# Token-major products with up to 512 columns from several column ranges, one PSUM bank for each token tile

## The chip, the cores and the metric

The kernel runs on one core of one Trainium2 chip. The metric is the device time of one execution in microseconds (us). A core has TensorE (PE in the profile; PEld are its weight loads), VectorE (DVE), ScalarE (ACT), GpSimd (POOL), and SyncE (SP), which here starts weight transfers.

## What is computed

Two blocks of two layers each, over 512 tokens of width 1024, batch 1. All arithmetic is float32 in the reference. Cut to what matters here:

```python
def first_block(x, ...):          # "layer A", twice
    for l in range(DEPTH):
        h = rms_norm(x, norm_g[l])
        p = h @ w_in[l]
        (cb, cc, cx, cgate, q, k, v, agate, iq, ik, iw, pu, pgate, mgate) = split_columns(p)
        y_a = short_conv_mixer(...)
        y_b = sparse_attention_mixer(q, k, v, agate, iq, ik, iw, ...)   # q, k: rms_norm per head of 64, then rope
        y_c = pool_mixer(...)
        x = x + merged @ w_o[l]

def second_block(x, mem, ...):    # "layer B" twice, each with cross attention and an MLP behind it
    for i in range(DEPTH):
        hn = rmsnorm(h, ln_mix[i])
        (aq, ak, av, hy, gq, gk, gv, go, glr, gates) = split_cols(hn @ w_in[i], IN_SPLITS_2)
        y_a = attention_mixer(aq, ak, av, ...) @ w_br_attn[i]
        y_b = hyena_mixer(hy, ...) @ w_br_hyena[i]
        y_c = gla_mixer(gq, gk, gv, go, glr, ...) @ w_br_gla[i]
        h = h + mixed @ w_out[i]
        h = h + memory_cross_attention(rmsnorm(h, ln_x[i]), rmsnorm(mem, ln_mem[i]), ...)
        h = h + jnp.square(jax.nn.relu(rmsnorm(h, ln_mlp[i]) @ mlp_w1[i])) @ mlp_w2[i]
```

The low-rank rows `glr` are 32 columns of layer B's input product; they give the decay of the gated linear attention (GLA).

## The kernel before

Every float32 product is made of three matmuls: both operands are split into a high part H and a remainder L, and `mm3` (L242 to L244) adds H·H, H·L and L·H in one PSUM bank. Weights are brought in pieces of four k-tiles (128 rows each) and 256 columns by `wload`: one transfer on SP into a raw buffer (`wr`, three of them), then ScalarE writes H (`wh`, three) and VectorE writes L (`wl`, two), 1024 columns at a time.

There are two forms of product. `gemm_t` keeps weights stationary and moves 512 tokens: its result has features on the partitions. `gemm_m` keeps tokens stationary and moves 256 weight columns: its result has tokens on the partitions ("token-major"), as queries, keys and values need it for norms and rope. A PSUM bank holds 512 float32 values per partition, so `gemm_m` puts two token tiles of 256 columns in one bank, and four token tiles take two banks. The pool `mm` has four banks, and each 256-column piece of either form takes two of them; while one piece's two banks are evicted, the next piece fills the other two.

Layer A (`layer_a`) makes the index queries with `gemm_m` (L642 and L644 in the listing), then in two chunks c the queries, keys and values by `q`, `k`, `v`; these products are put between others (`half`, and `between` in `gate_out`). `ev_q` and `ev_k` evict two token tiles at once: `sums64` squares on ScalarE and sums on VectorE, `rsqrt_small` takes the power -1/2 on GpSimd, `rope` runs on VectorE (L484, L486, L487), `split_hl` writes H and L. `ev_k` normalises first and turns afterwards (L675), so it waits for GpSimd.

Layer B starts with five token-major products in the order keys and values, q, half of the GLA values, q, the other half. `norm_full`, which scales the transposed input by the row norm, is queued behind the fourth. Then come weight-stationary products for the Hyena branch, interleaved with attention, and behind them the 32-column low-rank product (`ev_lr`), `gla_begin` (the decay), a 512-column product, and the GLA heads, which run as a background generator: `gla_steps` advances by one step at each half of a product, and `starts` says at which step each head begins. `gla_begin` begins with a memset (L1451); a head's first TensorE work are transposes of `kl`, written at L1521.

The cross attention makes keys and values of the 256 memory tokens (two token tiles) with `gemm_m`, four pieces of 256 columns each.

The code gives the operations and priorities; a scheduler of the framework then sets each engine's order when the kernel is built, by priority among what it holds ready. Weight loads and evictions have raised priority. `run_later` runs what was queued for the end of a product, as the turning of the cross keys.

Of the kernel before, what the change touches and what calls it, by code (L numbers as in the profile page):

```python
# [10 lines left out]
F32 = mybir.dt.float32  # L11
# [120 lines left out]
class Kernel:  # L132
# [309 lines left out]
    def rope_tables(self, base, g=None, axial=False):  # L442
# [3 lines left out]
        tb = self.tp.tile([P, 512], F32, tag="rt", name=self.nm("rt"), bufs=2)  # L446
        Atab = tb[:, : NT * 64].rearrange("p (t d) -> p t d", t=NT)
        Btab = tb[:, NT * 64 :].rearrange("p (t d) -> p t d", t=NT)
# [73 lines left out]
    def sums64(self, dst, src, nh):  # L522

        nc = self.nc
        sq = self.s2()[:, : 2 * nh * 64].rearrange("p (t h d) -> p t h d", t=2, h=nh)
        nc.scalar.activation(sq, src, AF.Square)
        nc.vector.tensor_reduce(dst, sq, AX.X, ALU.add)
# [65 lines left out]
    def layer_a(self, l, st, next_norm, side=None):  # L593
# [61 lines left out]
        def qkv(c):  # L655
# [5 lines left out]
            def ev_q(_, w, t, ps):  # L661
                src = ps.rearrange("p t (h d) -> p t h d", h=4)
                self.sums64(sigv[:, t : t + 2], src, 4)
                r = self.s2().rearrange("p (t h d) -> p t h d", t=2, h=4)
                self.rope(r, src, tabs_q, t, 4)
                self.split_hl(hls[0], r, t)

            def ev_k(_, w, t, ps):
                src = ps.rearrange("p t (h d) -> p t h d", h=4)
                sg = self.small(8, "sgk")  # L670
                sgv = sg.rearrange("p (t h) -> p t h", t=2)
                self.sums64(sgv, src, 4)
                self.rsqrt_small(sg, sg, 1.0 / 64, 8)
                kn = self.s2().rearrange("p (t h d) -> p t h d", t=2, h=4)
                nc.vector.tensor_tensor(kn, src, sgv.unsqueeze(3).to_broadcast([P, 2, 4, 64]), ALU.mult)  # L675
                r = self.s2().rearrange("p (t h d) -> p t h d", t=2, h=4)
                self.rope(r, kn, tabs_k, t, 4)
                self.split_hl(hls[1], r, t)
# [144 lines left out]
        half(1, [lambda: None] + steps)  # L823
# [430 lines left out]
    def layer_b(self, l, st, spec, next_norm):  # L1254
# [13 lines left out]
        tabs_q = self.rope_tables(self.axial_base, gains[:, 0:64], True)  # L1268
        tabs_k = self.rope_tables(self.axial_base, gains[:, 64:128], True)

        hlv = lambda t: t.rearrange("p a b -> p (a b)").rearrange("p (t h z d) -> p t h z d", t=NT, h=4, z=2)
        qhl, sigs = [], []
        kv = hlv(self.big())

        def sigma(dst, src, t, nt, nh, mul):

            bc = lambda a: a[:, t : t + nt].unsqueeze(2).to_broadcast([P, nt, nh])
            d3 = dst.rearrange("p (t h) -> p t h", t=nt)
            nc.vector.tensor_tensor(d3, src, bc(r2), ALU.mult)
            self.rsqrt_small(dst, dst, 1.0 / 64, nt * nh)  # L1280
            nc.vector.scalar_tensor_tensor(d3, d3, mul, bc(rstd), ALU.mult, ALU.mult)

        def ev_q(c, w, t, ps):
            if t == 0:
                qhl.append(hlv(self.big()))
                sigs.append(self.small(NT * 4, "sig"))
            src = ps.rearrange("p t (h d) -> p t h d", h=4)
            ss = self.small(8, "sgk")
            ssv = ss.rearrange("p (t h) -> p t h", t=2)
            self.sums64(ssv, src, 4)  # L1290
            sigma(sigs[-1][:, t * 4 : t * 4 + 8], ssv, t, 2, 4, 0.125)
            r = self.s2().rearrange("p (t h d) -> p t h d", t=2, h=4)
            self.rope(r, src, tabs_q, t, 4, True)
            self.split_hl(qhl[-1], r, t)

        def ev_kv(c, w, t, ps):
            src = ps[:, :, 0:P].rearrange("p t (h d) -> p t h d", h=2)
            ss = self.small(4, "sgk")
            ssv = ss.rearrange("p (t h) -> p t h", t=2)
            self.sums64(ssv, src, 2)  # L1300
            sigma(ss, ssv, t, 2, 2, 1.0)
            kn = self.s2()[:, :256].rearrange("p (t h d) -> p t h d", t=2, h=2)
            nc.vector.tensor_tensor(kn, src, ssv.unsqueeze(3).to_broadcast([P, 2, 2, 64]), ALU.mult)
# [94 lines left out]
        def ev_lr(j, w, ps):  # L1398
            for i in range(2):
                nc.scalar.activation(glr[i * 32 : i * 32 + 32], ps[:32], AF.Copy)  # L1400
# [438 lines left out]
```

## Time and profile before

| | us |
|---|---|
| median of 3 runs (lowest, highest) | 3375.7 (3374.16, 3376.68) |
| the profiled execution | 3377.46 |
| its span in the profile | 3375.7 |
| mean granted TensorE clock | 0.996 |
| VectorE busy | 2326.8 |

The span is the time from the first to the last profiled instruction. The granted clock is a share of full speed, 2.4 GHz. In a row of the timeline the first number is the start, the second the duration, and a bracket tells how long the engine was idle before and what released it. Matmuls are pipelined: a row's duration is longer than the distance to the next start.

### The profile page before, as it was taken

The page shows a single profiled execution, that of the slowest core. Times are in us where ns is not written, and L with a number is a line of the kernel's source. Part 1 is how long each engine was busy: PE and PEld are TensorE (multiplying, and loading weights), DVE is VectorE, ACT ScalarE, POOL GpSimd, SP SyncE. Part 2 cuts the span into 40 slices and gives each one's busy share as a digit, 9 for nine tenths or more (in the row PEclk, how much of TensorE's full clock was granted, in tenths as well). Part 3 has the DMA queues.
Part 4 walks back from the last instruction along what each step waited for, and adds up shares of the span by engine and source line. Part 5 has one row for each costly group of instructions (what it writes and reads, how often), then busy time and mean ns, then how long its engine had stood idle before and what let it go on. Part 6 is the DMA issues. An engine that isn't in the chain of part 4 may idle for free. (4 is left out here: it accounts for less than half of the span.)

```text
span 3375.7 us, 44852 instructions
## 1 busy us (share of the span) xinstructions
PE 3322.7 (98%) x16960; PEld 2774.1 (82%) x16960; DVE 2326.8 (69%) x4307; ACT 1484.0 (44%) x2455; POOL 301.2 (9%) x472
## 2 busy tenths in 40 slices
PE   8999999999999999999999999999999999999999
PEld 6888888888777887788888888889778888888887
DVE  7966645976778778778766666866876876653354
ACT  6254433435644356533344443344663334433222
POOL 1000000010111110011011101101000101000000
PEclk9999999999999999999999999999999999999999
DMA  5322334332345432235453434433222655233332
GB/s 138 94 76 75 89 112 130 84 95 69 89 118 153 145 80 74 80 100 172 137 177 96 130 123 126 142 120 99 77 80 68 179 149 173 94 125 95 99 114 88
DMA packets 331096, 376.36 MB, mean 111 GB/s; under 512 B 22558, under 2 KB 296852, under 8 KB 330880
## 3 DMA queue, kind: packets, MB, share of 16 engines
q1 hardware_dynamic: 298496, 294.72, 29.3%
q0 software_dynamic: 32384, 78.78, 8.0%
q8 instruction: 133, 2.18, 0.3%
q14 instruction: 83, 0.68, 0.1%
HBM read 340.93 MB, written 32.51 MB: 111 GB/s over the span
## 5 line engine op out<-in xcount | busy, mean ns | idle before, releaser
L242 PE MATMUL mm<-big,wh 128*128 128x512 f32 (+1 forms) x3496 | 1373.7, 393 | 5.7 <-ACT big L220 2.5
L243 PE MATMUL mm<-big,wh 128*128 128x512 f32 (+1 forms) x3496 | 1370.7, 392 | 2.3 <-DVE big L221 2.3
L244 PE MATMUL mm<-big,wl 128*128 128x512 f32 (+1 forms) x3496 | 1368.6, 392 | 0.0
L220 ACT ACTIVATE wh<-wr 128x1024 fp32r<-128x1024 f32 (+2 forms) x528 | 551.3, 1044 | 740.0 <-PE mm L243 516.7
L221 DVE TENSOR_TENSOR wl<-wr,wh 128x1024 fp32r<-128x1024 f32 (+2 forms) x528 | 635.1, 1203 | 291.7 <-PE mm L244 203.8
L242 PEld LDWEIGHTS mm<-big,wh 128*128 128x128 f32 (+1 forms) x3496 | 656.1, 188 | 150.1 <-ACT big L220 4.4
L243 PEld LDWEIGHTS mm<-big,wh 128*128 128x128 f32 (+1 forms) x3496 | 656.5, 188 | 141.7 <-DVE big L221 5.7
L244 PEld LDWEIGHTS mm<-big,wl 128*128 128x128 f32 (+1 forms) x3496 | 656.1, 188 | 137.1 <-issue 1.0
L242 PE MATMUL mm<-wh,big 128*128 128x256 f32 x1056 | 300.4, 284 | 0.0
L243 PE MATMUL mm<-wl,big 128*128 128x256 f32 x1056 | 299.9, 284 | 0.0
L244 PE MATMUL mm<-wh,big 128*128 128x256 f32 x1056 | 299.2, 283 | 0.0
L243 PEld LDWEIGHTS mm<-wl,big 128*128 128x128 f32 x1056 | 202.2, 191 | 1.1 <-DVE wl L221 0.2
L242 PEld LDWEIGHTS mm<-wh,big 128*128 128x128 f32 x1056 | 202.1, 191 | 0.9
L244 PEld LDWEIGHTS mm<-wh,big 128*128 128x128 f32 x1056 | 202.1, 191 | 0.2
L220 ACT ACTIVATE big<-s 128x512 fp32r<-128x512 f32 (+2 forms) x196 | 99.9, 530 | 150.3 <-DVE s L487 87.1
L221 DVE TENSOR_TENSOR big<-s,big 128x512 fp32r<-128x512 f32 (+2 forms) x196 | 107.3, 568 | 18.7 <-ACT big L220 17.0
L1749 DVE TENSOR_TENSOR s<-s 128x512 f32<-128x512 f32 x64 | 43.7, 688 | 103.2 <-ACT s L1748 103.2
L221 DVE TENSOR_TENSOR pt<-sd,pt 128x512 fp32r<-128x512 f32 (+3 forms) x160 | 87.8, 551 | 23.2 <-ACT pt L220 22.4
L220 ACT ACTIVATE pt<-sd 128x512 fp32r<-128x512 f32 (+3 forms) x160 | 76.8, 489 | 61.4 <-PE sd L307 49.3
L914 DVE TENSOR_TENSOR x<-mm,x 128x512 f32<-128x512 f32 x48 | 33.0, 688 | 76.9 <-PE mm L244 76.9
L307 PE MATMUL sd<-c,p 128*128 128x128 f32 x480 | 80.8, 278 | 2.9 <-DVE sm L565 1.2
L1748 ACT ACTIVATE s<-mm 128x512 f32<-128x512 f32 x64 | 37.5, 590 | 102.2 <-PE mm L244 102.2
(423 smaller groups left out, 3967.9 us busy)
## 6 DMA issues: line engine op xcount, KB each, us to landing
wr<-in_w_in_dram SPq DMA_DIRECT2D x244, 512.0 KB, 3.7
wr<-in_mlp_w_dram SPq DMA_DIRECT2D x128, 512.0 KB, 3.6
res<-x POOLq DMA_DIRECT2D x64, 256.0 KB, 2.9
x<-res POOLq DMA_DIRECT2D x48, 256.0 KB, 3.1
F<-spec SPq DMA_DIRECT2D x36, 256.0 KB, 3.7
wr<-in_w_o_dram SPq DMA_DIRECT2D x16, 512.0 KB, 3.5
wt<-in_c_dftf_dram POOLq DMA_DIRECT2D x32, 256.0 KB, 5.0
spec<-p POOLq DMA_DIRECT2D x32, 256.0 KB, 2.7
```

The source lines that it names most:

```text
L220: nc.scalar.activation(H, src, AF.Copy)
L221: nc.vector.tensor_tensor(L, src, H.bitcast(F32), ALU.subtract)
L242: mm(out, aH, bH, start=first, stop=False, **kw)
L243: mm(out, aH, bL, start=False, stop=False, **kw)
L244: mm(out, aL, bH, start=False, stop=last, **kw)
L307: self.nc.tensor.transpose(dst_ps[: s.shape[-1], i * P : i * P + s.shape[0]], s, self.ident)
L914: self.nc.vector.tensor_tensor(X, ps, X, ALU.add)
L1748: nc.scalar.activation(a, ps, AF.Relu)
L1749: nc.vector.tensor_tensor(a, a, a, ALU.mult)
```

## The change

A new `gemm_wide` takes a list of column ranges, together up to 512 columns, and gives each token tile a bank of its own: four token tiles take all four `mm` banks, two take two. A load (`wload_wide`) brings two of the eight k-tiles at full width, with one transfer for each range. For each load the code goes through the token tiles one by one. Evictions are called for one token tile after the other.

In layer A queries and keys of a chunk become one product (256 and 256 columns); one rope turns both from the raw product, and the keys are scaled by their norm afterwards. Values stay as they are. In layer B the five products become three: q with keys and values; q with half of the GLA values; the other half with the 32 low-rank columns (288 in all). The separate low-rank product goes; its rows, token-major, are turned by four transposes. `norm_full` is queued so that it comes one hand-over later than the next. The GLA heads start at steps 0, 5, 8, 11, and step 3 is skipped as well. In the cross attention keys and values are made in two pieces of 512 columns each. The diff, cut:

```diff
+    def wload_wide(self, segs, k0):
+        nc = self.nc
+        v = lambda t: t.rearrange("p a b -> p (a b)").rearrange("p (k n) -> p k n", k=2)
+        raw = v(self.wp.tile([P, 4, 256], F32, tag="wr", name=self.nm("wr"), bufs=3))
+        H = v(self.wp.tile([P, 4, 256], F32R, tag="wh", name=self.nm("wh"), bufs=3))
+        L = v(self.wp.tile([P, 4, 256], F32R, tag="wl", name=self.nm("wl"), bufs=2))
+        with self.tc.high_priority(offset=31000):
+            o = 0
+            for ap, c, w in segs:
+                nc.sync.dma_start(raw[:, :, o : o + w],
+                                  ap[k0 * P : (k0 + 2) * P, c : c + w].rearrange("(k p) n -> p k n", p=P))
+                o += w
+            self.split(H[:, :, :o], L[:, :, :o], raw[:, :, :o])
+        return H, L
+    def gemm_wide(self, segs, stat, evac, ntok=NT):
+        w = sum(s[2] for s in segs)
+        ps = [self.ps_mm() for _ in range(ntok)]
+        for kq in range(0, KD, 2):
+            H, L = self.wload_wide(segs, kq)
+            for t in range(ntok):
+                for k in range(2):
+                    aH, aL = stat(kq + k, t)
+                    self.mm3(ps[t][:, :w], aH, aL, H[:, k, :w], L[:, k, :w], kq + k == 0, kq + k == KD - 1)
+            if kq == KD // 2 - 2:
+                self.step_background()
+                self.run_later()
+        self.step_background()
+        self.run_later()
+        with self.tc.high_priority(offset=30000):
+            for t in range(ntok):
+                evac(t, ps[t])
...
+    def rope_pair(self, n, tag):
+        tb = [self.tp.tile([P, NT * n * 64], F32, tag=tag, name=self.nm("rt"), bufs=2) for _ in range(2)]
+        return [t.rearrange("p (t g d) -> p t g d", t=NT, g=n) for t in tb]
...
+            tabs_qk = self.rope_pair(2, "rt")
+            for i in range(2):
+                self.rope_tables(self.rope_base, gains[:, i * 64 : i * 64 + 64], into=[tb[:, :, i] for tb in tabs_qk])
...
+            def ev_qk(t, ps):
+                src = ps.rearrange("p (g h d) -> p g h d", g=2, h=4)
+                ss = self.small(8, "sgk")
+                self.sums64(ss, ps)
+                self.rsqrt_small(ss, ss, 1.0 / 64, 8)
+                nc.vector.tensor_scalar(sigv[:, t], ss[:, 0:4], 0.125, None, ALU.mult)
+                r = self.s2().rearrange("p (g h d) -> p g h d", g=2, h=4)
+                self.rope(r, src, [tb[:, t] for tb in tabs_qk], 0, 4)
+                nc.vector.tensor_tensor(r[:, 1], r[:, 1], ss[:, 4:8].unsqueeze(2).to_broadcast([P, 4, 64]), ALU.mult)
+                for i in range(2):
+                    self.split(hls[i][:, t, :, 0], hls[i][:, t, :, 1], r[:, i])
...
-            def q():
-                self.gemm_m(W, 2048 + c * 256, 256, KD, h_t, ev_q)
-                self.rsqrt_small(sig, sig, 1.0 / 64, NT * 4)
-                nc.vector.tensor_scalar(sig, sig, 0.125, None, ALU.mult)
-            k = lambda: self.gemm_m(W, 2560 + c * 256, 256, KD, h_t, ev_k)
+            qk = lambda: self.gemm_wide([(W, 2048 + c * 256, 256), (W, 2560 + c * 256, 256)], h_t, ev_qk)
             v = lambda: self.gemm_m(W, 3072 + c * 256, 256, KD, h_t, ev_v)
-            return [q, k, v], (hls, sigv)
+            return [qk, v], (hls, sigv)
...
-        half(1, [lambda: None] + steps)
+        half(1, [lambda: None, steps[0], lambda: None, steps[1]])
...
+        tabs = self.rope_pair(3, "rt3")
+        for i, o in enumerate((0, 0, 64)):
+            self.rope_tables(self.axial_base, gains[:, o : o + 64], True, into=[tb[:, :, i] for tb in tabs])
...
+        def heads(c, t, ps, ng):
+            n = ng * 2
+            src = ps[:, : n * 64]
+            ss = self.small(8, "sgk")[:, :n]
+            self.sums64(ss, src)
+            nc.vector.tensor_scalar(ss, ss, r2[:, t : t + 1], None, ALU.mult)
+            self.rsqrt_small(ss, ss, 1.0 / 64, n)
+            rs = rstd[:, t : t + 1]
+            nc.vector.tensor_scalar(sigs[c][:, t * 4 : t * 4 + 4], ss[:, :4], rs, 0.125, ALU.mult, ALU.mult)
+            v = lambda x: x.rearrange("p (g h d) -> p g h d", g=ng, h=2)
+            r = self.s2()[:, : n * 64]
+            self.rope(v(r), v(src), [tb[:, t, :ng] for tb in tabs], 0, 2, True)
+            r = r.rearrange("p (h d) -> p h d", h=n)
+            self.split(qhl[c][:, t, :, 0], qhl[c][:, t, :, 1], r[:, :4])
+            if n > 4:
+                nc.vector.tensor_scalar(ss[:, 4:6], ss[:, 4:6], rs, None, ALU.mult)
+                nc.vector.tensor_tensor(r[:, 4:6], r[:, 4:6], ss[:, 4:6].unsqueeze(2).to_broadcast([P, 2, 64]), ALU.mult)
+                self.split(kv[:, t, 0:2, 0], kv[:, t, 0:2, 1], r[:, 4:6])
...
-        self.gemm_m(W, 512, 256, KD, xg_t, ev_kv)
...
-        self.gemm_m(W, 0, 256, KD, xg_t, ev_q)
-        self.gemm_m(W, 2816, 256, KD, xg_t, ev_gv)
-        self.gemm_m(W, 256, 256, KD, xg_t, ev_q)
-        self.later.append(lambda: self.norm_full(st))
-        self.gemm_m(W, 3072, 256, KD, xg_t, lambda c, *a: ev_gv(c + 256, *a))
...
+        def ev_gl(t, ps):
+            rs = rstd[:, t : t + 1]
+            nc.scalar.activation(gv[:, t, 256:512], ps[:, 0:256], AF.Copy, scale=rs)
+            for i in range(2):
+                nc.scalar.activation(lr[:, t, i * 32 : i * 32 + 32], ps[:, 256:288], AF.Copy, scale=rs)
+            nc.vector.scalar_tensor_tensor(lr[:, t, 64:96], ps[:, 256:288], rs, lr[:, t, 0:32].bitcast(F32),
+                                           ALU.mult, ALU.subtract)
+        self.gemm_wide([(W, 0, 256), (W, 512, 256)], xg_t, ev_qkv)
+        self.gemm_wide([(W, 256, 256), (W, 2816, 256)], xg_t, ev_qg)
+        self.defer(lambda: self.norm_full(st), 2)
+        self.gemm_wide([(W, 3072, 256), (W, 3840, 32)], xg_t, ev_gl)
...
-        def ev_lr(j, w, ps):
-            for i in range(2):
-                nc.scalar.activation(glr[i * 32 : i * 32 + 32], ps[:32], AF.Copy)
-            nc.vector.tensor_tensor(glr[64:96], ps[:32], glr[:32].bitcast(F32), ALU.subtract)
+        def turn_lr():
+            tp = self.ps_sd()
+            self.transposes(tp, [lr[:, t].bitcast(F32) for t in range(NT)])
+            nc.scalar.copy(glr[:96], tp[:96])
...
-            self.gemm_t(W, 3840, 32, KD, h, ev_lr)
+            turn_lr()
...
-        starts, heads, n = (0, 4, 7, 10), [], 0
+        starts, heads, n = (0, 5, 8, 11), [], 0
         while n <= starts[-1] or heads:
             if n in starts:
                 heads.append(self.gla_head(starts.index(n), b, on, qk, gv, onrm, zt))
-            if n not in (1, 2):
+            if n not in (1, 2, 3):
...
+            self.gemm_wide([(A["x_wk_2"][l], c * 512, 512)], m_t, ev_k, NM)
+        keys(0)
+        keys(1)
...
-        self.gemm_m(A["x_wv_2"][l], 0, D, KD, m_t, ev_v, ntok=NM)
+        for c in range(2):
+            self.gemm_wide([(A["x_wv_2"][l], c * 512, 512)], m_t, partial(ev_v, c), NM)
```

## Rows read from the trace of the kernel before

**Rows 1.** Part 1 of the page: engine, busy us, share of the span, instructions.
```profile
PE 3322.7 (98%) x16960; PEld 2774.1 (82%) x16960; DVE 2326.8 (69%) x4307; ACT 1484.0 (44%) x2455; POOL 301.2 (9%) x472
```

**Rows 2.** Waits of TensorE: tile and line, releaser: us, times, longest.
```profile
PE sd L307 <- DVE gl L1521: 6.8, 2, 3.4
...
PE mm L242 <- ACT big L220: 2.5, 5, 0.9
```

**Rows 3.** Windows: stretch, length, busy us (instructions) of PE, PEld, DVE, ACT, POOL, clock.
```profile
1405.00:1420.00 15.00, 11.57 (x66) 9.28 (x65) 11.72 (x24) 8.78 (x15) 0.40 (x2) 0.89 0.25 72
2290.00:2330.00 40.00, 40.00 (x336) 40.00 (x335) 26.01 (x77) 15.06 (x29) 6.85 (x6) 1.00 0.34 98
```

**Rows 4.** TensorE by line and shape: count, busy us, mean ns, idle before.
```profile
L242 PE MATMUL mm<-wh,big 128*128 128x256 f32 x1056 | 300.4, 284 | 0.0
L243 PE MATMUL mm<-wl,big 128*128 128x256 f32 x1056 | 299.9, 284 | 0.0
...
L243 PE MATMUL mm<-big,wh 128*32 128x512 f32 x16 | 6.5, 404 | 0.0
```

**Rows 5.** Timeline of TensorE, 2310 to 2330, 169 rows: start, duration, instruction.
```profile
2309.73 0.28 PE L242 MATMUL mm<-wh,big 128*128 128x256 f32 x1
...
2329.89 0.28 PE L242 MATMUL mm<-wh,big 128*128 128x256 f32 x1
```

**Rows 6.** Timeline of TensorE, 3100 to 3120, 90 rows.
```profile
3099.74 0.39 PE L243 MATMUL mm<-big,wh 128*128 128x512 f32 x1
...
3119.91 0.39 PE L242 MATMUL mm<-big,wh 128*128 128x512 f32 x1
```

**Rows 7.** Timeline of VectorE, 2310.5 to 2319.5: an eviction in layer B.
```profile
2311.20 1.22 DVE L221 TENSOR_TENSOR wl<-wr,wh 128x1024 fp32r<-128x1024 f32 x1
...
2312.41 0.29 DVE L484 TENSOR_TENSOR s<-mm,rt 128x128 f32<-128x128 f32 x1
2312.61 0.17 DVE L532 TENSOR_SCALAR sig<-sig 128x8 f32<-128x8 f32 x1
...
2314.52 0.17 DVE L1281 SCALAR_TENSOR_TENSOR sig<-sig,rstd 128x8 f32<-128x8 f32 x1 [1.56 <-POOL sig L533]
...
2315.00 0.68 DVE L486 TENSOR_TENSOR s<-mm,rt 128x512 f32<-128x512 f32 x1
2315.60 0.68 DVE L527 TENSOR_REDUCE sgk<-s 128x8 f32<-128x512 f32 x1
...
2317.36 0.43 DVE L221 TENSOR_TENSOR big<-s,big 128x256 fp32r<-128x256 f32 x1
```

**Rows 8.** GpSimd by line and shape, 2265 to 2345.
```profile
L533 POOL TENSOR_TENSOR sig<-sig,c 128x8 f32<-128x8 f32 x4 | 6.5, 1636 | 28.4 <-DVE sig L532 28.4
...
L533 POOL TENSOR_TENSOR sgk<-sgk,c 128x4 f32<-128x4 f32 x2 | 2.0, 1004 | 4.3 <-DVE sgk L532 4.3
```

**Rows 9.** Timeline of VectorE, 264 to 272: an eviction in layer A.
```profile
265.29 0.69 DVE L675 TENSOR_TENSOR s<-mm,sgk 128x512 f32<-128x512 f32 x1 [1.82 <-POOL sgk L533]
```

**Rows 10.** Timeline of TensorE: a short wait, and the GLA wait with what follows.
```profile
948.11 0.47 PE L1056 MATMUL sd<-wt,hA 128*128 128x512 f32 x1 [1.29 <-DVE hA L1042]
...
1410.48 1.12 PE L307 MATMUL sd<-c,gl 128*128 128x128 f32 x4 [3.40 <-DVE gl L1521]
...
1411.82 0.63 PE L243 MATMUL mm<-big,wh 128*128 128x512 f32 x1
1412.25 0.63 PE L244 MATMUL mm<-big,wl 128*128 128x512 f32 x1
```

**Rows 11.** Timeline of TensorE, 2346 to 2359: first and last of four waits.
```profile
2346.82 0.50 PE L243 MATMUL mm<-big,wh 128*128 128x512 f32 x1 [0.37 <-DVE big L221]
...
2358.59 0.50 PE L1337 MATMUL sd<-t,t 128*128 128x512 f32 x1 [0.73 <-ACT t L498]
```

**Rows 12.** Timeline of VectorE, 1368 to 1379: where the GLA chain begins.
```profile
1368.69 0.48 DVE L1451 MEMSET p<- 96x512 f32 x1
```

More of the change, by code (lines that the diff above doesn't have):

```diff
@@ L520, in p2, with sums64 @@
         return self.pp.tile([P, 512], dt, tag="p2", name=self.nm("p2"))
-    def sums64(self, dst, src, nh):
+    def sums64(self, dst, src):
         nc = self.nc
-        sq = self.s2()[:, : 2 * nh * 64].rearrange("p (t h d) -> p t h d", t=2, h=nh)
+        n = src.shape[1] // 64
+        sq = self.s2()[:, : n * 64]
         nc.scalar.activation(sq, src, AF.Square)
-        nc.vector.tensor_reduce(dst, sq, AX.X, ALU.add)
+        nc.vector.tensor_reduce(dst, sq.rearrange("p (h d) -> p h d", h=n), AX.X, ALU.add)
     def rsqrt_small(self, dst, src, mul, n):
@@ L1267, in layer_b @@
         self.tp = scope.enter_context(self.tc.tile_pool(name=f"tb{l}", bufs=6, reuse_waits="tile"))
-        tabs_q = self.rope_tables(self.axial_base, gains[:, 0:64], True)
-        tabs_k = self.rope_tables(self.axial_base, gains[:, 64:128], True)
+        tabs = self.rope_pair(3, "rt3")
+        for i, o in enumerate((0, 0, 64)):
+            self.rope_tables(self.axial_base, gains[:, o : o + 64], True, into=[tb[:, :, i] for tb in tabs])
         hlv = lambda t: t.rearrange("p a b -> p (a b)").rearrange("p (t h z d) -> p t h z d", t=NT, h=4, z=2)
-        qhl, sigs = [], []
+        qhl = [hlv(self.big()) for _ in range(2)]
@@ L1273, in layer_b @@
+        sigs = [self.small(NT * 4, "sig") for _ in range(2)]
         kv = hlv(self.big())
[L1275 to L1303, printed above, removed]
-            r = self.s2()[:, :256].rearrange("p (t h d) -> p t h d", t=2, h=2)
-            self.rope(r, kn, tabs_k, t, 2, True)
-            self.split_hl(kv[:, :, 0:2], r, t)
-            for i in range(2):
-                vs = ps[:, i, P : 2 * P].rearrange("p (h d) -> p h d", h=2)
-                self.split(kv[:, t + i, 2:4, 0], kv[:, t + i, 2:4, 1], vs, scale=rstd[:, t + i : t + i + 1])
@@ L1622, in cross, with keys, ev_k, turn @@
         kH, kL = v8(self.big()), v8(self.big())
-        def ev_k(c, w, t, ps):
-            hd = c // 256
-            ss = self.small(2, "mmr")
-            for i in range(2):
-                sq = self.s2()
-                nc.scalar.activation(sq[:, :256], ps[:, i], AF.Square, accum_out=ss[:, i : i + 1])
-            self.rsqrt_small(ss, ss, 1.0 / 256, 2)
-            kn = self.s2()
-            for i in range(2):
-                nc.vector.tensor_scalar(kn[:, i * 256 : (i + 1) * 256], ps[:, i], ss[:, i : i + 1], None, ALU.mult)
-            def turn():
+        def keys(c):
+            kn = []
+            def ev_k(t, ps):
+                ss = self.small(2, "mmr")
+                for i in range(2):
+                    sq = self.s2()
+                    nc.scalar.activation(sq[:, :256], ps[:, i * 256 : (i + 1) * 256], AF.Square, accum_out=ss[:, i : i + 1])
+                self.rsqrt_small(ss, ss, 1.0 / 256, 2)
+                k = self.s2()
+                for i in range(2):
+                    sl = slice(i * 256, (i + 1) * 256)
+                    nc.vector.tensor_scalar(k[:, sl], ps[:, sl], ss[:, i : i + 1], None, ALU.mult)
+                kn.append(k)
+                if t == NM - 1:
+                    self.later.extend([partial(turn, 0), partial(turn, 1)])
+            def turn(n):
+                hd = c * 2 + n
                 tp = self.ps_sd()
-                self.transposes(tp, [kn[:, t_ * 256 + i * P : t_ * 256 + (i + 1) * P] for i in range(2) for t_ in range(NM)])
+                o = n * 256
+                self.transposes(tp, [kn[t][:, o + i * P : o + (i + 1) * P] for i in range(2) for t in range(NM)])
                 with self.tc.high_priority(offset=30000):
@@ L1678, in cross, with ev_v @@
         V = []
-        def ev_v(c, w, t, ps):
-            if c == 0:
+        def ev_v(c, t, ps):
+            if c == 0 and t == 0:
                 V.extend([vv(self.big()), vv(self.big())])
-            self.split(V[0][:, :, c : c + 256], V[1][:, :, c : c + 256], ps)
+            sl = slice(c * 512, (c + 1) * 512)
+            self.split(V[0][:, t, sl], V[1][:, t, sl], ps)
         oH, oL = [None, None], [None, None]
```

51 lines of the change are left out of this document (19 added, 32 removed).

## The prediction

> **What bounds the kernel now.** I read four views, from the widest to the narrowest. Part 1 of the page: TensorE is busy for 3322.7 us, VectorE for 2326.8, ScalarE for 1484.0 [rows 1]. Little can come from waiting less; the time falls only if TensorE gets less to do, and rises wherever a change makes it wait. Second, TensorE's waits: the largest that comes back twice is the 3.4 us before the GLA heads' first transposes, and the longest into an ordinary product is 0.9 us [rows 2]. No row names an eviction that had not given its PSUM bank back, which is where this change will reach. Third, the table of stretches: over the 40 us of layer B's token-major products TensorE works 40.00 of 40.00 us at a granted clock of 1.00, while VectorE works 26.01 and GpSimd 6.85 [rows 3]. So those products are bound by the stream of matmuls, with their evictions hidden. Fourth, the groups by shape: three groups of 1056 matmuls with 256 moving columns, which is all the token-major work, and the 32-column low-rank products, three groups of 16 [rows 4].
>
> **Part 1: wider products.** Of the 3168 matmuls with 256 columns, 288 (index queries) and 384 (layer A's values) stay. The other 2496 change: 768 in layer A's q and k (2 layers, 2 chunks, 2 products of 8 x 4 x 3), 960 in layer B (2 layers, 5 products of 96), 768 in the cross keys and values. In a stretch without waits the 169 rows from 2309.73 to 2329.89 start 20.16/168 = 0.1200 us apart [rows 5]; with 512 columns the 90 rows from 3099.74 to 3119.91 start 20.17/89 = 0.2266 us apart [rows 6]. A pair of the narrow kind costs 0.2400, so one wide one saves 0.0134. I use spacings and not the durations of the groups, since neighbours overlap. For 288 columns no row exists: between 0.1200 and 0.2266; I take 1/8 of the way, 0.1333, because the columns are 32 of 256 more.
> Before: 2496 x 0.1200 = 299.5 us. After: 1152 x 0.2266 = 261.0, and 192 x 0.1333 = 25.6, together 286.6. Saved: 12.9 us (the unknown 288 between 15.5 and -5.0). All of it lies on TensorE, the bound.
> The Trainium skill, "TensorE: Matmul & The Clock Gate", section "Back-to-back issue gap", gives N/2.4 + 2.5 ns as the isolated gap of a warm matmul; by that a pair saves only 2.5 ns. The rows show 13.4.
>
> **Part 2: the low-rank rows.** 48 matmuls of 512 columns (only 32 of 128 stationary columns used [rows 4]) at the spacing of rows 6 are 10.9 us. Their columns now ride in the 288 counted above. Added: 8 transposes of 128 columns, each at most a 256-column matmul's 0.1200, at least nothing: 1.0 taken. Net on TensorE: 12.9 + 10.9 - 1.0 = 22.8 us saved.
>
> **Part 3: banks.** This is the price. A narrow product holds two of four `mm` banks, so the next one starts in the other two. A wide product with four token tiles holds all four, and what follows waits for evictions. VectorE's rows overlap their neighbours by 0.08 us (2315.00 + 0.68 against 2315.60), so I cost one at its duration less 0.08: 512 elements 0.60, 256 0.35, 128 0.21, small 0.09, a weight split 1.14 [rows 7]. GpSimd's power takes 1.64 us for 8 elements, 1.00 for 4 [rows 8], and VectorE has stood behind it for 1.56 and 1.82 us [rows 7, 9].
> Layer A, q and k together, four exits. One token tile: sum of squares 0.60, two small 0.18, rope 2 x 0.35 + 2 x 0.60 = 1.90, scaling 0.35, two splits 0.70: 3.7 us. Reading the raw product for rope frees the bank before the power is back. Tile 0 ends 3 x 6 x 0.2266 = 4.1 us ahead of the product, so its bank is free at about 0.1 us behind the end; with a share of weight splits (1.14) the others follow at about 5.0, 9.1, 13.5. The next product does two loads' worth of matmuls on its first bank, 12 x 0.2266 = 2.7 us, then needs the second at 5.0. Wait 2.2 in strict order, less where the builder's scheduler finds a third ready load: 1.6 taken, 6.4 in all.
> Layer B, qkv to qg, two exits: per tile 3.4 us of VectorE (axial rope in four 128-wide or 192-wide pieces), releases at 0.1, 4.95, 8.55, 12.15; each tile of the follower has 2.7 us of work before it needs a third load. Gaps: 4.95 - 2.8 = 2.1, then 0.9, then up to 0.9: 2.8 to 4.0, I take 3.4, so 6.8.
> qg to gl, two exits: per tile 2.2 us, releases at -1.0, 1.9, 4.65, 7.4 against 12 x 0.1333 = 1.6 us of work per tile: 0.3 + 1.15 + 1.15 = 2.6, within 1.5 to 3, I take 2.2, so 4.4.
> Cross keys and values have two token tiles, hold two banks, and stay double-buffered: no wait, and the cover is the other pair of banks; without it each exit would cost about a layer A one, 1.6.
> Sum: 17.6 us. Bounds: nothing (rows 3 show exits with no wait at all), and strict load order (every load wants all four tiles before the next), where a follower stops after one load on tile 0: layer A 4.3, qkv 8.1, qg 5.0 each, so 17.2 + 16.2 + 10.0 = 43.4. I take the lower middle because the order of instructions is set by what the builder holds ready, and it has two loads ahead.
>
> **Part 4: what moves.** norm_full is put off by one more hand-over, to the end of gl; its consumers now wait at four places of a layer, the first for 0.37 and the last for 0.73 us [rows 11], some 2 us in all. Put off to where VectorE has the short evictions of gl and not two of q's rope beside it, it should cost half: 1.0 less per layer, 2.0 in all (bounds: nothing, 2 x 2 us).
> The GLA chain begins when attention ends (the memset at 1368.69 [rows 12]), not when the low-rank product ends; that product, 24 x 0.2266 = 5.4 us per layer, was cover for TensorE until 1410.48. The heads' start positions move by one half step, which is half of a 512-column product's 48 matmuls, 24 x 0.2266 = 5.4, and give it back. Cost 0; if it doesn't come back, 5.4 per layer. The wide loads of two ranges add one DMA on SP each (10 wide products in A and B, 40 loads); no row of TensorE waits for a weight DMA, and wr has three buffers, so 0. If that cover were gone, a load's wait would be bounded by the longest weight wait of any product, below 1 us [rows 2].
>
> **Sum.** -22.8 + 17.6 - 2.0 = -7.2. Against the profiled execution, 3377.5 (span 3375.7 and 1.8 around it), that is 3370.3; that execution lies 1.8 above the median 3375.7, so **3368.5** against the median.
>
> **Rivals.** *R1, the banks cost half or less*: the next product's matmuls on freed banks cover the evictions. For it: rows 3 (VectorE has 14 of 40 us free). Half: 3375.7 - 22.8 + 8.8 - 2.0 = 3359.7; nothing at all: 3350.9.
> *R2, slower: strict load order.* If the follower stops at every bank, 43.4 us of waits come in place of 22.8. A wait also costs clock: behind 3.40 us of idling the matmuls start 0.43 us apart for a while (1411.82, 1412.25), TensorE's 1.2 GHz level, behind 1.29 us at 948.11 they don't [rows 10]; the stretch 1405:1420 has a mean clock of 0.89, 0.11 x 15 = 1.65 us [rows 3]. Six such falls: 9.9. 3375.7 - 22.8 + 43.4 - 2.0 = 3394.3, with clock 3404.2. It decides once waits pass 24.8 us.
> *R3, the columns save nothing*: rows 6 are of weight-stationary products; if a wide token-major matmul took as long as the pair that it replaces, 0.2400, the 12.9 would be lost: 3381.4. Only the fixed part of a matmul could be saved, and the skill page of Part 1 makes that small; the two spacings of rows 5 and 6 speak against it.
> *R4, short waits throttle the clock*: eight exits, each with one loss of 1.65, +13.2: 3381.7. For: rows 10 at 3.40 us. Against: the 1.29 us wait cost nothing. The Trainium skill, same page, section "A second HAM failure mode: psum-queue depth-cycling", says that small idles between groups of matmuls, as PSUM banks are cycled, make the clock swing; no row here shows it for such short waits.
> *R5, the GLA cover isn't given back*: 2 x 5.4 = 10.9 more, 3379.4.
>
> **How the numbers follow.** The forecast, 3364 to 3374 by its own bounds (layer A 1.4 to 2.2, qkv 2.8 to 4.0, qg 1.5 to 3.0), gets 0.42, of which 0.26 below 3369 and 0.16 above. R1 0.24, R2 0.16, R3 0.05, R4 0.07, R5 0.06. A measurement of this kernel tells about 0.2%, 6.8 us, from no change. Faster 0.26 + 0.24 = 0.50; same 0.16 + 0.05 + 0.07 + 0.06 = 0.34; slower 0.16. The range leaves out R2 and a little of R1: 3351 to 3386.
>
> **What would show it.** Right: 512-column token-major matmuls 0.227 us apart; TensorE's busy time about 20 us less; new waits of 1 to 4 us in `mm` products released by VectorE or ScalarE lines of rope, at four places in layer A and four in B; none in cross; the GLA wait near 3.4. Wrong: no `mm` wait at all (R1), waits of 4 us and more followed by 0.43 us spacing (R2), a GLA wait near 9 (R5), 0.240 us spacing (R3). The forecast fails most easily in Part 3, whose order I infer.

## The result, and the profile after

The change makes the kernel slower: 3399.5 us median (3397.2 to 3403.4) against 3375.9 for the kernel before beside it, a ratio of 1.0072 (95% interval 1.0054 to 1.0089). The forecast was 3368.5, in a range that ended at 3386. The profiled execution took 3399.45 us, its span is 3397.4.

TensorE's row of part 1 of the page after, to be laid beside [rows 1]:

```profile
PE 3312.3 (97%) x15768; PEld 2711.6 (80%) x15768; DVE 2335.3 (69%) x4405; ACT 1492.9 (44%) x2473; POOL 301.5 (9%) x480
```

TensorE is busy 10.4 us less, where about 20 was forecast, and the span is 21.7 us longer, so it stands idle 32 us more. The waits of TensorE in the kernel after (tile and line, releaser: us in total, times, longest) say where:

```profile
PE mm L242 <- DVE s L530: 9.3, 8, 1.9
...
PE mm L242 <- DVE sgk L1317: 6.4, 2, 3.2
PE mm L242 <- ACT big L1342: 6.4, 6, 1.5
PE sd L343 <- DVE gl L1554: 4.4, 2, 2.2
...
PE sd L409 <- DVE s L402: 3.3, 2, 1.7
...
PE mm L242 <- DVE big L224: 2.3, 2, 1.2
...
PE mm L242 <- DVE s L776: 1.7, 2, 1.2
...
PE mm L243 <- DVE wl L221: 1.6, 3, 0.7
PE mm L242 <- DVE s L769: 1.3, 2, 0.8
```

In the kernel before no row of that view named an eviction that reads a bank of a token-major product [rows 2]. Now L530 (rope; all eight waits lie in layer A), L224 (the split of the values in qkv) and L1342 (the scaling of the GLA values in qg) hold TensorE for 24.4 us. In this sum is the row of L1317: L1317 reads no bank, it is VectorE's next instruction behind L224. Another 8 us stand at row sums of the norm (L402), layer A's other evictions (L776, L769) and weight splits (wl). The GLA wait, before 6.8 [rows 2], is 4.4.

A second reading needs no releaser: the start of one and the same matmul in both traces. Before the change the first L1056 of the filters behind a 1.29 us wait stands at 948.11 [rows 10]; after it is this row, L1090 by the new numbering:

```profile
962.84 0.47 PE L1090 MATMUL sd<-wt,hA 128*128 128x512 f32 x1 [1.26 <-DVE hA L1076]
```

It is 14.7 us later. Taken so, at matmuls that all these programs have, the distance grows like this (the last two columns are variants, below):

| at, in the trace of before | after - before, us | x4 - before, us | x8 - before, us |
|---|---|---|---|
| 596, first layer A done | +6.2 | -1.8 | -2.9 |
| 948, second layer A done | +14.7 | -0.9 | -4.0 |
| 1175, layer B begins | +11.3 | -0.3 | -6.6 |
| 1521, first layer B's GLA done | +17.3 | +4.5 | -7.5 |
| 2280, layer B begins again | +17.0 | +3.9 | -8.0 |
| 2644, second GLA done | +23.4 | +8.3 | -10.2 |
| 3370, end | +21.8 | +7.3 | -12.2 |

Both layers A and both layers B lose; the stretches with the cross attention win a little, as do the filters between 948 and 1175. These are single executions; their ends differ from the medians below by up to 4 us.

### The profile page after: what moved, and what is told of

It is laid out like the page before. It is cut to its first block, busy times and chain, and to the rows that moved or that the text cites. A ratio compares the mean times of both kernels' runs of the same rounds, so it can differ in the third digit from the quotient of the medians.

```text
span 3397.4 us, 42740 instructions
## 1 busy us (share of the span) xinstructions
PE 3312.3 (97%) x15768; PEld 2711.6 (80%) x15768; DVE 2335.3 (69%) x4405; ACT 1492.9 (44%) x2473; POOL 301.5 (9%) x480
## 5 line engine op out<-in xcount | busy, mean ns | idle before, releaser
L220 ACT ACTIVATE wh<-wr 128x1024 fp32r<-128x1024 f32 (+1 forms) x528 | 551.7, 1045 | 811.4 <-PE mm L243 541.8
L221 DVE TENSOR_TENSOR wl<-wr,wh 128x1024 fp32r<-128x1024 f32 (+1 forms) x528 | 635.0, 1203 | 328.1 <-PE mm L244 219.7
L242 PE MATMUL mm<-wh,big 128*128 128x512 f32 (+2 forms) x672 | 236.5, 352 | 16.5 <-DVE sgk L1317 6.4
L243 PE MATMUL mm<-wl,big 128*128 128x512 f32 (+2 forms) x672 | 234.6, 349 | 1.6 <-DVE wl L221 1.6
L244 PE MATMUL mm<-wh,big 128*128 128x512 f32 (+2 forms) x672 | 233.5, 348 | 0.0
L220 ACT ACTIVATE big<-s 128x512 fp32r<-128x512 f32 (+1 forms) x196 | 103.8, 534 | 125.9 <-DVE s L531 61.9
L242 PEld LDWEIGHTS mm<-wh,big 128*128 128x128 f32 x672 | 127.6, 190 | 36.9 <-ACT big L1342 8.2
L243 PEld LDWEIGHTS mm<-wl,big 128*128 128x128 f32 x672 | 127.6, 190 | 17.4 <-DVE wl L221 3.1
L244 PEld LDWEIGHTS mm<-wh,big 128*128 128x128 f32 x672 | 127.3, 190 | 14.9
L221 DVE TENSOR_TENSOR big<-s,big 128x512 fp32r<-128x512 f32 (+1 forms) x196 | 109.4, 568 | 17.4 <-ACT big L220 16.0
L220 ACT ACTIVATE pt<-sd 128x512 fp32r<-128x512 f32 (+3 forms) x160 | 76.9, 489 | 73.5 <-PE sd L343 61.1
L221 DVE TENSOR_TENSOR pt<-sd,pt 128x512 fp32r<-128x512 f32 (+3 forms) x160 | 88.1, 552 | 27.7 <-ACT pt L220 26.7
L343 PE MATMUL sd<-c,p 128*128 128x128 f32 x480 | 80.7, 277 | 2.7 <-DVE p L611 1.3
```

The source lines that it names most:

```text
L220: nc.scalar.activation(H, src, AF.Copy)
L221: nc.vector.tensor_tensor(L, src, H.bitcast(F32), ALU.subtract)
L242: mm(out, aH, bH, start=first, stop=False, **kw)
L243: mm(out, aH, bL, start=False, stop=False, **kw)
L244: mm(out, aL, bH, start=False, stop=last, **kw)
L343: self.nc.tensor.transpose(dst_ps[: s.shape[-1], i * P : i * P + s.shape[0]], s, self.ident)
```

## The experiments

All times are medians of 4 to 10 runs beside runs of the kernel before on the same chip (3375.9 to 3378.0); the ratios are to those, and a difference told below is to those too.

| kernel | us | ratio to before (95%) |
|---|---|---|
| after | 3399.5 | 1.0072 (1.0054, 1.0089) |
| x1_only_a | 3392.7 | 1.0044 (1.0029, 1.0059) |
| x2_only_b | 3388.6 | 1.0035 (1.0020, 1.0049) |
| x3_only_cross | 3375.4 | 0.9994 (0.9985, 1.0003) |
| x4_power_later | 3383.7 | 1.0017 (1.0008, 1.0026) |
| x5_copy_out | 3388.3 | 1.0034 (1.0021, 1.0047) |
| x6_lowrank_back | 3411.6 | 1.0104 (1.0089, 1.0119) |
| x7_copy_and_power | 3381.0 | 1.0015 (1.0005, 1.0025) |
| x8_two_phases | 3368.0 | 0.9974 (0.9964, 0.9983) |
| y1_before_sigma_later | 3378.8 | 1.0007 (0.9997, 1.0016) |
| y2_after_power_twice | 3435.6 | 1.0173 (1.0158, 1.0188) |
| y3_phases_power_twice | 3366.8 | 0.9972 (0.9962, 0.9982) |
| y4_phases_gla_later | 3373.8 | 0.9991 (0.9982, 1.0001) |

**One part at a time: x1, x2, x3.** Each takes the functions of one part from the kernel after and the rest from before:

```
x1: layer_a of after;            layer_b, gla_steps, cross of before
x2: layer_b, gla_steps of after; layer_a, cross of before
x3: cross of after;              layer_a, layer_b, gla_steps of before
```

> Only layer A has the wide product of queries and keys; layer B, the GLA starts and the cross attention are as before. Theory B (a product on four banks makes what follows wait for the evictions): the two traces stand 7.2 us apart over the first layer A and 8.5 over the second, and 3.5 come back behind them, so some 12 us above before, about 3388. Rival L (the loss is the removed low-rank cover and the moved GLA heads): no loss here, the columns' 5.1 us gained, about 3371.

> Only layer B has its wide products, the low-rank columns in gl and the new GLA starts; layer A and the cross attention are as before. Theory B: the traces part by 6.6 and 7.1 us over the two layers B, about 13.5 above before, 3389. Rival L: the whole 23 us, 3399.

> Only the keys and values of the cross attention are made 512 columns wide, in two banks. 768 matmuls at 0.1200 become 384 at 0.2266: 5.1 us less work. Theory B: no bank is short, so 3.7 to 5.1 us below before, 3371 to 3372. If wide token-major matmuls were no faster: 3376, no change.

Against before on the same chip they are 14.7 and 10.6 us longer and 2.6 shorter, together 22.7, and the whole change is 23.5: the parts add up. Rival L, by which all of the loss lay in layer B, falls with x1. x3's matmuls save 5.1 us; the 2.6 us measured are not clear of noise (0.9985 to 1.0003). Between its wide products TensorE now waits for a weight remainder once in each layer B, 1.03 and 0.67 us; the list of TensorE's waits before has no such row:

```profile
1746.31 0.50 PE L243 MATMUL mm<-wl,big 128*128 128x512 f32 x1 [1.03 <-DVE wl L221]
```

**What holds the bank: x4.** The timeline of VectorE in the kernel after, in layer A's eviction of queries and keys (L577 prepares the power, L528 and L530 are rope and read the bank, L712 is the query scale):

```profile
167.95 0.16 DVE L577 TENSOR_SCALAR sgk<-sgk 128x8 f32<-128x8 f32 x1
...
169.89 0.17 DVE L712 TENSOR_SCALAR sig<-sgk 128x4 f32<-128x4 f32 x1 [1.45 <-POOL sgk L578]
169.97 0.69 DVE L530 TENSOR_TENSOR s<-mm,rt 128x512 f32<-128x512 f32 x1
...
175.48 0.17 DVE L712 TENSOR_SCALAR sig<-sgk 128x4 f32<-128x4 f32 x1 [1.09 <-POOL sgk L578]
...
175.89 0.68 DVE L530 TENSOR_TENSOR s<-mm,rt 128x512 f32<-128x512 f32 x1
```

L530 needs nothing from GpSimd, but L712 does, and it stands ahead of L530 in VectorE's queue: 1.45 and 1.09 us in which the bank's last reader waits for a scalar that it doesn't use. In layer B a wait of 1.28 us stands ahead of rope too (L1320, L530), but there rope isn't the bank's last reader. The values lie in the same bank, and their split (L224) comes behind the heads' work. Rope has read the first tile's bank at 1204.29, the product ends at 1204.42, and TensorE goes on only behind L224:

```profile
1203.43 0.23 DVE L1320 TENSOR_SCALAR sig<-sgk,rstd 128x4 f32<-128x4 f32 x1 [1.28 <-POOL sgk L578]
...
1203.74 0.55 DVE L530 TENSOR_TENSOR s<-mm,rt 128x384 f32<-128x384 f32 x1
...
1207.13 0.34 DVE L224 SCALAR_TENSOR_TENSOR big<-mm,rstd,big 128x128 fp32r<-128x128 f32 x1
```

TensorE at that place:

```profile
1207.62 0.77 PE L242 MATMUL mm<-wh,big 128*128 128x512 f32 x1 [3.21 <-DVE sgk L1317]
```

x4 moves that line behind rope, in both evictions:

```diff
-                nc.vector.tensor_scalar(sigv[:, t], ss[:, 0:4], 0.125, None, ALU.mult)
                 r = self.s2().rearrange("p (g h d) -> p g h d", g=2, h=4)
                 self.rope(r, src, [tb[:, t] for tb in tabs_qk], 0, 4)
+                nc.vector.tensor_scalar(sigv[:, t], ss[:, 0:4], 0.125, None, ALU.mult)
```

> The kernel after, with one line moved in each of the two evictions: the query scales, which need GpSimd's power, are written behind rope and not ahead of it. In the trace of after VectorE stands 0.8 to 1.45 us behind the power in each token tile with the bank's last reader (rope) queued behind. Theory P (this wait sets when banks come free): the releases come 1 us sooner per tile, some 2 us of wait less at each of 8 exits, about 3383. Rival W (VectorE's own work for four tiles sets it, the power is hidden in it anyway): within 3 us of after, 3399.

3383.7: 5.7 above before where the whole change was 23.5 above. The same place in x4 (L530 is rope's last reading of the bank, L714 the query scale):

```profile
167.36 0.68 DVE L530 TENSOR_TENSOR s<-mm,rt 128x512 f32<-128x512 f32 x1
168.90 0.17 DVE L714 TENSOR_SCALAR sig<-sgk 128x4 f32<-128x4 f32 x1 [0.86 <-POOL sgk L578]
...
173.05 0.68 DVE L530 TENSOR_TENSOR s<-mm,rt 128x512 f32<-128x512 f32 x1
```

The wait is still there, 0.86 us, now behind the reader. The waits on L530 fall from 9.3 us to 2.8, and by the table above the layers A lose nothing any more (-0.9 at 948). Layer B still waits for banks:

```profile
PE mm L242 <- ACT big L1342: 5.2, 4, 1.4
PE mm L242 <- DVE big L224: 4.6, 2, 2.3
...
PE mm L242 <- DVE s L530: 2.8, 4, 0.8
```

Both evictions of values, L224 and L1342, are untouched by x4. In VectorE's timeline of x4, in qkv, the query scale (L1324 there) now stands behind rope, but it and its wait are still ahead of L224:

```profile
1191.82 0.23 DVE L1324 TENSOR_SCALAR sig<-sgk,rstd 128x4 f32<-128x4 f32 x1 [0.65 <-POOL sgk L578]
...
1194.69 0.35 DVE L224 SCALAR_TENSOR_TENSOR big<-mm,rstd,big 128x128 fp32r<-128x128 f32 x1
```

**Does the power's time itself set the loss: y2, y3, and the control y1.** y2 and y3 let GpSimd take a second power, with exponent 1, in the wide evictions only; the results stay as they are.

```diff
-        nc.gpsimd.tensor_tensor(dst, dst, self.mhalf[:, :n], ALU.pow)
+        for e in [self.mhalf, self.ones][: 2 if again else 1]: nc.gpsimd.tensor_tensor(dst, dst, e[:, :n], ALU.pow)
```

> The kernel after with GpSimd's power in the wide evictions followed by a second one with exponent 1, so 1.64 us more for 8 elements, 1.0 for 4, per token tile, and no more work for VectorE, ScalarE or TensorE. Theory P: VectorE stands that much longer ahead of the bank's last reader, so each exit's waits grow by one to three times that: 15 to 30 us above after, 3415 to 3430. Rival W (VectorE's amount of work sets the releases): within 4 us of after.

> x8 (two phases) with the same second power. Theory P: nothing that waits for the power stands ahead of a bank's last reader, so no more than 4 us above x8, 3368 to 3372. If the power delays the bank in some other way (GpSimd's queue, buffers of the sums): as much as in the kernel after.

y2 is 3435.6, 36 us above after and more than expected; y3 is 3366.8, no slower than x8. So the same added GpSimd time costs 36 us where a bank's reader is queued behind it and nothing where it isn't. In y2 VectorE's rows grow by the power's time and the first two last readers are 7.64 us apart in place of 5.92:

```profile
172.73 0.17 DVE L712 TENSOR_SCALAR sig<-sgk 128x4 f32<-128x4 f32 x1 [3.17 <-POOL sgk L578]
172.81 0.69 DVE L530 TENSOR_TENSOR s<-mm,rt 128x512 f32<-128x512 f32 x1
...
180.04 0.17 DVE L712 TENSOR_SCALAR sig<-sgk 128x4 f32<-128x4 f32 x1 [2.81 <-POOL sgk L578]
...
180.45 0.68 DVE L530 TENSOR_TENSOR s<-mm,rt 128x512 f32<-128x512 f32 x1
```

y1 is the control in the kernel before, where a narrow product leaves two banks free:

```diff
-            sigma(sigs[-1][:, t * 4 : t * 4 + 8], ssv, t, 2, 4, 0.125)
             r = self.s2().rearrange("p (t h d) -> p t h d", t=2, h=4)
             self.rope(r, src, tabs_q, t, 4, True)
+            sigma(sigs[-1][:, t * 4 : t * 4 + 8], ssv, t, 2, 4, 0.125)
```

> The kernel before, with the same move as in x4: in layer B's query evictions the sum's scaling, the power and the query scale are written behind rope. Control: with narrow products two of four banks stay free for the next product. Theory P as stated (a wait of VectorE on the power costs only where four banks are held): no change, 3376 within 3. Rival (the power's wait costs in any eviction): some 1.5 us at each of 8 evictions, 3364 to 3370.

No change that can be measured. In y1's timeline a wait of 1.56 us on GpSimd still stands in this eviction, behind the first two tiles' rope. In the kernel before it was there too (1.56 us in [rows 7]), and TensorE worked 40.00 of 40.00 us around it [rows 3]: with two banks free it cost nothing.

**Free the banks early: x5, x7, x8.** x5 has ScalarE copy each bank out before anything else (of qg only the queries; there the values are read from the bank next), and rope works on the copy, in place; x7 is x5 with x4's move.

```diff
-            def ev_qk(t, ps):
+            def ev_qk(t, bank):
+                ps = self.s2()
+                nc.scalar.copy(ps, bank)
```

> The kernel after, but ScalarE first copies each bank of the q and k evictions (512 columns in layer A and in qkv, 256 in qg) to SBUF, and everything else reads the copy; the order of the power is that of after. Theory B (waits for banks that an eviction holds): a bank is free one ScalarE copy (0.59 us) after its last matmul, whatever VectorE does, so the 31 us of waits on releases by L530, L1317, L1342, L224 and the following ones vanish but for about a third: some 15 to 20 us below after, 3380 to 3384. Rival W (VectorE's backlog itself reaches TensorE by late weight splits and late evictions of the products behind): within 5 us of after.

> The copy of x5 and the moved line of x4 together. Theory B with P as its price: what x4 left of bank waits (3.4 us in layer A, some 12.5 in layer B) goes too: 3368 to 3373, below the kernel before. Rival W: no better than x4, 3384.

Both gained less than expected: 12.1 and 4.7 us above before. x7 is no better than x4 by more than noise (1.0015 and 1.0017), as its rival had it. The timeline of ScalarE in x7, at the end of qkv, shows why (L1335 is the copy that frees a bank, L220 a split):

```profile
1185.78 0.59 ACT L1335 COPY s<-mm 128x512 f32<-128x512 f32 x1 [0.25 <-PE mm L244]
...
1187.14 0.59 ACT L1335 COPY s<-mm 128x512 f32<-128x512 f32 x1 [0.21 <-PE mm L244]
...
1192.53 0.31 ACT L220 ACTIVATE big<-s 128x128 fp32r<-128x128 f32 x1 [1.61 <-DVE s L1330]
1192.75 0.57 ACT L1335 COPY s<-mm 128x512 f32<-128x512 f32 x1
...
1196.12 0.77 ACT L220 ACTIVATE big<-s 128x256 fp32r<-128x256 f32 x2 [1.96 <-DVE s L531]
1196.80 0.57 ACT L1335 COPY s<-mm 128x512 f32<-128x512 f32 x1
```

The first two copies start 1.36 us apart, as their products end. The third comes 5.6 us behind the second, right behind a split that waited 1.61 us for VectorE, the fourth behind one that waited 1.96. In these rows ScalarE too works through its queue in order, and a copy behind such a split frees nothing early. (The copies also take four of the six `s2` buffers; how much of the delay that is, was not told apart.)

x8 needs no copy. Evictions return what is left to do, and `gemm_wide` calls that only when all four tiles have been through rope. In layer B it also moves the values' evictions ahead of the heads' work, so that rope becomes the last reader of every bank; the buffers for the sums (`sgk`) are four in place of two:

```diff
-                evac(t, ps[t])
+            for f in [evac(t, ps[t]) for t in range(ntok)]:
+                if f is not None:
+                    f()
...
                 self.rope(r, src, [tb[:, t] for tb in tabs_qk], 0, 4)
+                def rest():
+                    nc.vector.tensor_scalar(sigv[:, t], ss[:, 0:4], 0.125, None, ALU.mult)
...
+                return rest
...
         def ev_qkv(t, ps):
-            heads(0, t, ps, 3)
             vs = ps[:, 384:512].rearrange("p (h d) -> p h d", h=2)
             self.split(kv[:, t, 2:4, 0], kv[:, t, 2:4, 1], vs, scale=rstd[:, t : t + 1])
+            return heads(0, t, ps, 3)
...
         def ev_qg(t, ps):
-            heads(1, t, ps, 2)
             nc.scalar.activation(gv[:, t, 0:256], ps[:, 256:512], AF.Copy, scale=rstd[:, t : t + 1])
+            return heads(1, t, ps, 2)
```

> x4, and the evictions in two phases: first for all four token tiles what reads the bank (squares, sums, rope), then for all four the rest (query scales, key scaling, splits). No copy, no work added. Per tile VectorE has 2.6 us ahead of the release in place of 3.7 in layer A, about 2.5 in place of 3.4 in layer B. Theory B: 3 tiles times about 1 us at six exits, of which half is wait: about 8 us below x4, 3375. Rival W: same as x4.

3368.0, a ratio of 0.9974: 8.3 us below before, and some 32 below the whole change. The last readers of the four banks of qkv in VectorE's timeline of x8 (L531 there):

```profile
1185.16 0.54 DVE L531 TENSOR_TENSOR s<-mm,rt 128x384 f32<-128x384 f32 x1
...
1188.82 0.54 DVE L531 TENSOR_TENSOR s<-mm,rt 128x384 f32<-128x384 f32 x1
...
1191.59 0.54 DVE L531 TENSOR_TENSOR s<-mm,rt 128x384 f32<-128x384 f32 x1
...
1193.85 0.54 DVE L531 TENSOR_TENSOR s<-mm,rt 128x384 f32<-128x384 f32 x1
```

They are 3.66, 2.77 and 2.26 us apart. In the kernel after the last readers of the same banks, the rows of L224, start at 1207.13, 1210.82, 1215.88 and 1222.51, and the first ends 3.1 us behind the product. In x8 TensorE has no wait at all between 1174 and 1232, over qkv, qg and gl. Its waits in the whole trace:

```profile
PE sd L1572 <- DVE gl L1554: 6.5, 4, 3.0
...
PE mm L242 <- ACT big L220: 3.0, 5, 1.0
...
PE mm L242 <- ACT gl L1436: 2.8, 2, 1.4
```

No eviction of q, k or their values is left among the first rows. By the table x8 gains 3 us on x4 over the layers A, where there are only the two phases, and 12 over the layers B up to the GLA's end. There the two phases and the values' move were not told apart.

**The low-rank rows and the GLA: x6, y4.** x6 is the kernel after with `gemm_t(W, 3840, 32, ...)` and `ev_lr` back, gl 256 columns wide, and the old GLA starts. y4 is x8 with one more step skipped:

```diff
-            if n not in (1, 2, 3):
+            if n not in (1, 2, 3, 4):
```

> The kernel after with the low-rank product taken back out of gl (256 columns wide, low-rank rows by their own 48 matmuls, GLA starts 0, 4, 7, 10). Theory: the low-rank part alone is a gain of 10.9 - 2.6 (32 columns more in 192 matmuls) - 1.0 less the two GLA waits' growth of some 3, so this kernel is 3 to 7 us above after, 3403 to 3406. Rival L (the cover is missing behind it): below after, by up to 10.

> x8, and the GLA's step 4 is skipped too, so the first head's TensorE work comes one half-step (24 matmuls, 5.4 us) later. In x8 TensorE waits 3.0 us twice for it, as it did for 3.4 before the change. Theory: the wait is the missing cover between gla_begin and the first head, so it goes: 5 to 6 us below x8, 3362. Rival: the heads' end then lacks cover and gives it back, 3368 or above.

x6 lies further above before than the kernel after does (1.0104 against 1.0072, some 11 us), so in this kernel the low-rank part is a gain, and a larger one than the 3 to 7 expected; what the rest of it is was not followed up. Its GLA wait is that of the kernel before again:

```profile
PE sd L343 <- DVE gl L1548: 7.2, 2, 3.6
```

y4 missed: 3373.8, above x8. The first head's wait of 3.0 us went from its waits, but these came:

```profile
PE mm L242 <- ACT big L220: 7.4, 4, 3.3
...
PE mm L244 <- DVE wl L221: 3.9, 2, 2.0
```

Products wait 7.4 us for L220 where they waited 3.0 in x8, and 3.9 for weight remainders. The rival's number came, its reason (what a head gains in cover at its beginning it lacks later) only in part: in the first layer B a wait of 1.94 us for weights stands at the heads' beginning, at 1405.80, where x8 waited 2.99 at 1404.26, and one of 3.26 us for L220 behind the heads, at 1637.95, where x8 waited 0.96.

## Why the prediction was wrong

**Part 1 held** in its spacings. Timeline of TensorE in the kernel after, two wide token-major matmuls inside qg:

```profile
2333.68 0.39 PE L244 MATMUL mm<-wh,big 128*128 128x512 f32 x1
...
2335.72 0.39 PE L244 MATMUL mm<-wh,big 128*128 128x512 f32 x1
```

The same view, two 288-column ones inside gl:

```profile
1240.03 0.29 PE L243 MATMUL mm<-wl,big 128*128 128x288 f32 x1
...
1241.47 0.30 PE L242 MATMUL mm<-wh,big 128*128 128x288 f32 x1
```

Ten rows of the first kind, 2.04/9 = 0.227 us apart; twelve of the second, 1.44/11 = 0.131, against 0.2266 and 0.1333 in the sum. R3 is out. **Part 2 held** in its matmuls and was a gain beside x6; in x8 its gain doesn't show (below).

**Part 3 failed, in the size of its term.** Where the waits would come was right: layer A's exits, qkv to qg, qg to gl. The releasers are rope in layer A, as forecast, but the evictions of the values in layer B. That the follower goes on to its next load was right too: between the waits at 2328.82 and 2337.57, behind the second qkv exit, TensorE's timeline has 26 matmuls, where a stop at every load would have let 6 through. What was mis-sized is the 17.6 us. Per layer A the traces part by 7.2 (from -1.0 at 75 to 6.2) and 8.5 us, to which the 2.6 us of saved columns (384 x 0.1200 - 192 x 0.2266) are added: 9.8 and 11.1, or about 5.2 an exit, where the sum had 1.6. Per layer B they part by 6.0 and 6.4 us where the sum, with 12.5 us less work for both layers (columns, low-rank product, transposes) and 3.4 + 2.2 - 1.0 of waits in each, had -1.7 each. Three steps are behind it:

- "Reading the raw product for rope frees the bank before the power is back." It didn't. I took from the data that rope doesn't need the power; in the rows of x4 above VectorE takes its instructions in the order in which they were put, and the query scale was ahead. The rows to see it on were in front of me: VectorE standing for GpSimd [rows 7, 9]. Layer A's banks come free 0.2, 6.1, 11.8 and 18.0 us behind the product's end (170.43), where I had 0.1, 5.0, 9.1 and 13.5; in x4 it is 1.4 before the end and 4.3, 9.3 and 14.0 behind it. x4 gives 18 of the 23.5 us back by this alone, by the table nearly all of it in the layers A; y2 and y3 confirm it from the other side.
- In qkv I had the first bank free 0.1 us behind the product's end, as if rope were its last reader. Rope had read it by then, but the values' split read the same bank until 3.1 us behind the end, and TensorE waited 3.21 us.
- The eviction's other work (adding, scaling, splits) was priced per tile, but its place between the tiles was not questioned. x8 puts it behind all four, and the values ahead, and gains 14 us more (5.7 above before to 8.3 below).

Behind these, waits came in other rows: 8 us in the norm, in layer A's other evictions and in weight splits, which a sum over the exits alone doesn't have.

**The savings were too large as well.** x8 shows no wait for a bank at these exits, so by the sum it would be where R1 has no waits at all, at 3350.9; it is at 3368.0. Of the 24.8 us of Parts 1, 2 and 4 some 8 are left there. So of the 31 us by which the forecast missed some 14 are Part 3's (the banks cost some 31, after against x8, in place of 17.6), and some 17 are savings that didn't arrive, unless the order of x8 itself costs some of them. TensorE's busy time, forecast to fall by about 20 us, fell by 10.4 in the kernel after and by 16.7 in x8 (to 3306.0). One place is layer B behind the token-major products. The same piece of the program, before and in x8 (length, busy times, clock):

```profile
1250.00:1521.00 271.00, 264.97 (x1376) 213.24 (x1375) 204.68 (x410) 142.38 (x243) 18.04 (x32) 0.99 0.30 85
1240.40:1513.50 273.10, 264.29 (x1362) 213.56 (x1361) 204.81 (x409) 142.17 (x243) 18.00 (x32) 0.99 0.31 84
```

The first has the low-rank product's 24 matmuls, priced at 5.4 us, the second hasn't, and it is 2.1 us longer. New waits as that on L1436 (1.40 us there) are a part of it; the cause stays open.

Three readings were off. The whole list behind [rows 2] has a weight wait of 1.3 us, in the first product, where the prediction bounded it by 1, and it names two evictions of weight-stationary products, 1.2 us on L791 and 0.5 on L1384, where the prediction saw none. And the axial rope has pieces of 96 and 64 columns (L528 in VectorE's timeline after, 0.25 and 0.22 us a row), not 128 or 192.

**Part 4.** Cross attention was given no wait; x3 gained 2.6 us of 5.1, not clear of noise, with 1.7 us of waits for weights. norm_full's waits (L221 and L498 as releasers, 3.8 us in the list of before) are gone after, but 3.3 us came at the norm's row sums (L402). The GLA wait stayed near 3.4 as said: 2.2 at the heads' transposes (L343), with up to 1.5 new at another line of the heads (L1563 behind L1545). R5 is out.

**The rivals.** The time fell into R2's span, 3394 to 3404, but not by R2's way, the strict load order: the follower did go on to the next load. That the numbers meet is luck. R2's point of decision held: TensorE's idle time grew by 32 us, past 24.8. R4 is out as the main loss; the clock fell behind some waits only (below). R1 is out for this kernel. x8, with the banks freed early, lies at 3368.0, where the forecast had put the change itself; that is a coincidence: smaller savings, but no waits for banks.

## What to carry to other kernels

Before a product may hold all banks of a pool, look at the queue of the engine that evicts it: the bank comes free when the last instruction that reads it has run, and everything that stands ahead of that one counts, a wait for a third engine's scalar above all. Look for all readers of the bank: in layer B the last was not rope but the split of the values beside it. A wait that cost nothing while other banks were free is then on the path. Put the readers of all banks first and the rest behind them; here that turned a loss of 23.5 us into a gain of 8.

## What the runs showed of the hardware

TensorE's clock fell behind shorter waits than I had counted with. Behind 1.79 us at 176.72 the matmuls went on 0.23 us apart; behind 1.87 us at 281.44 they went to 0.43:

```profile
281.44 0.47 PE L242 MATMUL mm<-big,wh 128*128 128x512 f32 x1 [1.87 <-DVE s L530]
...
282.36 0.63 PE L242 MATMUL mm<-big,wh 128*128 128x512 f32 x1
282.79 0.63 PE L243 MATMUL mm<-big,wh 128*128 128x512 f32 x1
```

The two stretches around them, length, busy times, clock:

```profile
170.00:185.00 15.00, 12.84 (x56) 9.98 (x55) 12.58 (x30) 5.89 (x11) 4.63 (x3) 1.00 0.24 70
278.00:293.00 15.00, 13.13 (x51) 10.38 (x51) 11.35 (x29) 6.04 (x11) 5.47 (x4) 0.89 0.29 81
```

Granted clocks of 1.00 and 0.89 in 15 us each: a fall to 1.2 GHz costs some 0.11 x 15 = 1.65 us, nearly as much as the wait ahead of it. Over the whole trace this stayed small: the mean granted clock is 0.995 after and 0.996 before, which of these spans is 17.0 and 13.5 us, so some 3 us more.

The Trainium skill, "TensorE: Matmul & The Clock Gate", section "A second HAM failure mode: psum-queue depth-cycling", says that short idles between groups of matmuls, as banks are cycled, make the clock swing. The trace agrees at 281.44, and not at 176.72; of the loss it was a small part.
